# Two-block transformer kernel on one core: bias rows in 32 copies instead of 128, memory tokens loaded earlier, nine weight pages instead of seven at the start

## Chip, core and metric

The kernel runs on one core of a Trainium2 chip. The metric is the device time of one execution in microseconds (us); of several runs the median counts. Engines are named as in the profile: PE (TensorE matmul), PEld (its weight loads), DVE (VectorE), ACT (ScalarE), POOL (GpSimd), SP (SyncE); a "q" behind a name is the engine's instruction queue, where DMAs are issued.

## What is computed

Two blocks on 256 tokens of width 1024, in float32 throughout. Cut to what this case touches, the first block is:

```
h    = rms_norm(x) @ w_in            # q, k, v of two attentions, 512 columns each
oa   = softmax(qa ka^T / 8 + bias[h, bucket(t - s)], causal) va        # 8 heads of 64
ob   = (softmax(.. + bias) - lam * softmax(.. + bias)) vb              # 4 heads, two maps each
x    = x + concat(norm(oa), norm(ob)) @ w_out
m    = rms_norm(mem)                 # 256 memory tokens
x    = x + softmax((rms_norm(x) wq)(m wk)^T) (m wv) wo
x    = x + swiglu(rms_norm(x))
```

The bias of a head depends on the distance t - s alone, so that a row of 384 numbers per head holds all of a head's 256x256 map. A second block follows (gated linear recurrence, spatial gating, routing to 8 of 64 experts) and the final norm; the change leaves both as they are.

## The kernel before

All work is unrolled and its order is the program's order on every engine. SBUF is cut into 25 **pages** of 1 MB (128 partitions x 2048 float32).

**Chunks.** The weights come as a planned stream of 1 MB pages (class Stream, L175 to L274); I call the n-th page of the plan chunk n. Chunks 0 to 11 are w_in, two per 512 columns, in the order k, q, v of the first attention (0 to 5) and k, q, v of the second (6 to 11); chunks 12 to 15 are w_ck, 16 to 19 w_cv, then w_out and the rest. A chunk is loaded (L220), then **converted** by halves: ACT rounds it into a page `wh` (L246) and DVE forms the rest `wl` (L247), two pages in all, and the raw page is free again. A product is three matmuls: with `wh` (L643), with the low part of the other side (L644), with `wl` (L645). A chunk is 48 matmuls of 256 columns (tile `ws`) or 24 of 512 (tile `tsb`).

**What sets the order.** `st.limit(name)` takes from the table CAP (L81) how many pages the stream may hold and how many half chunks may stand converted ahead. `pump` (L202) converts half a chunk if there is room for two pages, then issues loads as long as there is room for one page, and for two more if a loaded chunk is still unconverted (L210). It is called at every `get`, in the middle of a chunk and at every `free`. "start" holds from the beginning until "a1" (3 pages, L983), which is set behind chunk 11; "a2" (7 pages, L975) is set between chunks 13 and 14. At a `free` under "start" the stream of before holds two converted chunks and issues one load.

**Queues.** All loads named here are issued by SP, in program order; the store of the bias rows is issued by ACT. Every DMA of both queues gets one of eight completion semaphores in turn, and one that gets a semaphore again is not issued before the transfer that had it last has landed. So a transfer that takes long holds back the eighth DMA after it, and on the same queue all that stand behind that one.

**The bias.** PE forms the 12 rows of 384 numbers (`bv`, L710), DVE copies them to SBUF (L711), and one DMA writes every row 128 times to DRAM (`bd`, L715) at a pitch of 513, so that reading at a pitch of 512 from offset 127 turns copy p by p places: partition p of the map. Two loads (L778) fetch the maps, `biasA` for 8 heads and `biasB` for 4, behind chunk 5. The store stands on ACT's queue behind the first two of four quarter steps, each of which scales two blocks of xT (`gain`, L580/L581) and converts a quarter of chunk 0 (L575/L576).

**Attention.** The weave "att" (L980) puts the attention steps, the preparation of the memory tokens (`mem_prep`, L897) and the second attention between the half chunks of chunks 6 to 19, at the places in ORDER (L43). The scores `qk` of the first attention come in the middle of chunk 7, the softmax (L809 adds the bias, L811 takes the maximum, L813 the exponentials) behind them, the transposes `pt` (L832) behind chunk 8. The loads of memT and mem (L892, L894) are issued behind the bias maps; they are first read by `mem_prep` in the middle of chunk 8.

```
 210  if src is None or self.room() < 1 + (2 if self._pending() else 0): break
 237  if 2 * self.ready >= self.ahead and force is None or self.room() < 2: break
```

Of the kernel before, what the change touches and what calls it, by code (L numbers as in the profile page):

```python
# [10 lines left out]
F32 = mybir.dt.float32  # L11
# [16 lines left out]
def steps():  # L28
# [7 lines left out]
    for kind in KINDS:  # L36
# [41 lines left out]
        [-1, -1, -1, 3],  # L78
    ],
}  # L80
CAP = {"start": (7, 4), "a1": (3, 8), "a2": (7, 4), "a3": (9, 4), "a4": (11, 3), "out": (10, 2), "cq": (9, 4),  # L81
       "cq1": (8, 5), "cross": (7, 3), "co": (10, 4), "ffn": (12, 3), "ffn_in": (10, 5), "z": (8, 5), "f0": (5, 4),
       "f1": (8, 4), "v": (6, 4), "cm": (6, 4), "gt": (8, 6), "branch": (12, 2), "wo": (14, 4), "post": (11, 3),
       "router": (18, 3)}
# [90 lines left out]
class Stream:  # L175
# [19 lines left out]
    def limit(self, name):  # L195
        self.cap, self.ahead = CAP[name]
        self.pump()
# [83 lines left out]
def run_all(gen):  # L281
    for _ in gen:
        pass
# [40 lines left out]
def body(nc, tc, A, OUT, ctx, dbg=None):  # L324
# [8 lines left out]
    dr = ctx.enter_context(tc.tile_pool(name="dr", bufs=1, space=bass.MemoryType.DRAM))  # L333
    ctx.enter_context(tc.manual_schedule())

    def raw_page(name, dt=F32):
        return pg.tile([128, 2048], dt, tag="pg", name=name, bufs=NP)

    def page(name, dt=F32):
        assert len(live) + st.used + 1 <= NP, (name, [n for n, _ in live.values()], st.used)  # L340
        t = raw_page(name, dt)
        live[id(t)] = (name, t)
        return t
# [15 lines left out]
    def bank(name="bk"):  # L359
        return ps.tile([128, 512], F32, tag="ps", name=name, bufs=8)  # L360
# [23 lines left out]
    def w3(t, **kw):  # L384
        return t.rearrange("p (a b) -> p a b", **kw)
# [78 lines left out]
    oh, bvs = tmp0[0:33, 0:384], tmp0[0:12, 384:768]  # L464
# [35 lines left out]
    def gcol(key):  # L500
        a, n = COL[key]
        return [cols[:, i:i + 1] for i in range(a, a + n)]
# [36 lines left out]
    def rstd2(src, junk):  # L539
        return newton(sumsq(halves(src), halves(junk)), 2, 1024.0)  # L540
# [33 lines left out]
    def split(hi, lo, src):  # L574
        S.activation(hi, src, AF.Copy)  # L575
        V.tensor_sub(lo, src, hi.bitcast(F32))  # L576
# [6 lines left out]
    def gain(parts, xT_, g, ks=range(8)):  # L583

        for k in ks:
            sl = slice(k * 256, k * 256 + 256)
            split_scaled(parts[0][:, sl], parts[1][:, sl], xT_[:, sl], g[k])
# [54 lines left out]
    def mm3(out, l, r, start, stop, free=False):  # L642
        PE.matmul(out, l[0], r[0], start=start, stop=False, skip_group_check=free)  # L643
        PE.matmul(out, l[0], r[1], start=False, stop=False, skip_group_check=free)  # L644
        PE.matmul(out, l[1], r[0], start=False, stop=stop, skip_group_check=free)  # L645


    def ws512(hT, key, c0, evac, need=None):

        hv = [w3(h, a=8) for h in hT]  # L650
        bks = [bank("ws") for _ in range(2)]
        for h in range(2):
            if need:
                need(h)
            c = st.get((key, c0, h))
            wv = [w3(x, a=4) for x in (c.hi, c.lo)]
            for k in range(4):
                for ct in range(4):
                    o = bks[ct // 2][:, (ct % 2) * 256:(ct % 2) * 256 + 256]
                    mm3(o, [x[:, k, ct * 128:ct * 128 + 128] for x in wv], [x[:, h * 4 + k, :] for x in hv],  # L660
                        h == 0 and k == 0 and ct % 2 == 0, h == 1 and k == 3 and ct % 2 == 1, True)
                if k == 1:
                    st.pump()
                    yield
            st.free(c)
            if h == 0:
                yield
        for i in range(2):
            evac(i, bks[i])
        yield  # L670
# [34 lines left out]

    st.cap, st.ahead = CAP["start"]
    c.hi, c.lo = raw_page("wh", F32R), raw_page("wl", F32R)
# [1 line left out]
    bv = bank("bv")  # L709
    PE.matmul(bv[0:12, 0:384], tab, oh, start=True, stop=True)  # L710
    V.tensor_copy(bvs, bv[0:12, 0:384])  # L711
    bd = dr.tile([12, 128, 512], F32, name="bd")
    for i in range(4):
        if i == 2:
            nc.scalar.dma_start(bass.AP(tensor=bd.tensor, offset=bd.offset, ap=[[65536, 12], [513, 128], [1, 384]]),  # L715
                                bvs[:, None, :].to_broadcast([12, 128, 384]))
        s = slice(i * 512, i * 512 + 512)
        gain(hT, xT, gcol("mix_norm_g"), (2 * i, 2 * i + 1))
        split(c.hi[:, s], c.lo[:, s], c.raw[:, s])
# [15 lines left out]
    def evac_q(dst, f):  # L735
        def g(i, b):
            V.scalar_tensor_tensor(w3(dst[:, i * 512:i * 512 + 512], a=2), w3(b, a=2), 0.125, f["row"][:, None, :]
                                   .to_broadcast([128, 2, 256]), op0=OP.mult, op1=OP.mult)
        return g
# [9 lines left out]
    next(unit), next(unit)  # L749
    fx["col"] = rstd2(xp, mixed)  # L750
    run_all(unit)
    unit = ws512(hT, "w_in", 0, evac_q(qkA[:, 0:1024], fx))
    next(unit), next(unit)
    fx["row"] = row_of(fx["col"])
# [20 lines left out]
    rel(tmp0)  # L775
    run_all(ts512(hT, "w_in", 1024, evac_v(vab[:, 0:1024], fx)))
    for t, h0, n in ((biasT[0], 0, 8), (biasT[1], 8, 4)):
        nc.sync.dma_start(w3(t[:, :n * 256], a=n), bass.AP(tensor=bd.tensor, offset=bd.offset + h0 * 65536 + 127,  # L778
                                                           ap=[[512, 128], [65536, n], [1, 256]]))

    def attention(diff, qk_, v, bias, out_cols):
        q, k = w3(qk_[:, 0:1024], a=4), w3(qk_[:, 1024:2048], a=4)
# [105 lines left out]
        yield from turns(mixed, fm["mx"], 8, (gcol("moba_out_g") + gcol("diff_subln_g") * 4), bs=(2, 3) if diff else (0, 1))  # L888


    memT = page("memT")
    nc.sync.dma_start(memT, A["memT"])  # L892
    memx = page("mem")
    nc.sync.dma_start(memx, A["mem"])  # L894
    fm = {}

    def mem_prep():  # L897
# [236 lines left out]
    def ffn_in():  # L1134
        hv = [w3(h, a=8) for h in nh["h"]]
        for u in range(11):
# [4 lines left out]
            for n in ("w_gate", "w_up"):  # L1141
# [3 lines left out]
                for k in range(8):  # L1145
# [5 lines left out]
                    if k == 3:  # L1151
# [18 lines left out]
                                                ap=[[0, 128], [1, 1024]]))  # L1170
# [6 lines left out]
    for u in range(11):  # L1177
# [3 lines left out]
        for tt, k2 in sorted(parts) if u == 10 else parts:  # L1181
            f = 2 * u + k2
            i, o = divmod(f * 256, 2048)
# [977 lines left out]
    bd = [mset.bank("ed") for n in range(2)]  # L2161
# [88 lines left out]
```

## Time and profile before

| | |
|---|---|
| median of 3 runs | 1227.41 us (1226.05 to 1227.77) |
| the profiled execution | 1227.2 us, its span 1225.4 us |
| PE busy, DVE, ACT | 95%, 52%, 38% of the span |
| DMA moved | 353.20 MB, mean 288 GB/s |

The page's busy shares are means over stages that differ much: weights with conversion (to about 757 us), then the experts. A stretch view (from:to in us, busy time and count of each engine, granted clock PEclk, busy share of the DMA engines, GB/s) shows each stage by itself. In a timeline row the first two numbers are start and duration, and square brackets tell the idle time of the engine before it and what ended it. [...]

### The profile page before, as it was taken

To read this page: it belongs to the slowest core of one execution; us is meant where nothing else is said; L and a number is where in the kernel's file an instruction comes from. 1 tells how busy PE (TensorE), PEld (TensorE's weight loads), DVE (VectorE), ACT (ScalarE), POOL (GpSimd) and SP (SyncE) were. 2 spreads that over 40 slices of the span, in tenths; PEclk is the share of its full clock that TensorE was granted. 3 is DMA by queue.
4 is the path that set the end of the run, shared out by engine and by line. 5 is a ranking of instruction groups with operands and counts; after the bars stand their busy time and mean duration, and the time that the engine had idled before them with its cause. 6 is when DMAs were issued, how large, how long until landed. Compare 5 with 4: busy or idle time off the path is not lost.

```text
span 1225.4 us, 18528 instructions
## 1 busy us (share of the span) xinstructions
PE 1166.3 (95%) x7391; PEld 837.5 (68%) x7391; DVE 632.9 (52%) x1280; ACT 465.9 (38%) x738; POOL 2.0 (0%) x9
## 2 busy tenths in 40 slices
PE   7989999999999999999999978999999999998986
PEld 6878987689999988998888757444444434442442
DVE  4568856465545446865686656343333323331333
ACT  4446535545534443777445433111111111110121
POOL 0000000000000000000000000000000000000000
PEclk9889999999999999999999988999999999999998
DMA  8853789644554665343355997899999999999994
GB/s 300 252 213 138 264 344 388 241 174 153 190 206 143 228 226 178 118 149 114 139 193 197 361 359 288 336 410 422 422 420 420 421 421 421 420 421 421 421 420 175
DMA packets 55152, 353.20 MB, mean 288 GB/s; under 512 B 6007, under 2 KB 9368, under 8 KB 13848
## 3 DMA queue, kind: packets, MB, share of 16 engines
q1 hardware_dynamic: 51984, 342.90, 70.7%
q10 hardware_dynamic: 3080, 9.10, 2.6%
q8 instruction: 59, 0.97, 0.3%
q14 instruction: 29, 0.24, 0.1%
HBM read 347.51 MB, written 4.46 MB: 287 GB/s over the span
## 4 chain that ended last, share of the span: by engine, by line
PE 70%; DMA 22%; DVE 4%; ACT 2%; issue 1%; SPq 0%; DVEq 0%; ACTq 0%
DMA w<-in_w_expert_gu 11%; PE gu L1940 8%; DMA w<-in_w_expert_down 6%; PE tsb L643 6%; PE tsb L645 6%; PE tsb L644 6%; PE ed L1969 5%; DMA w<-in_w_in 3%; PE ga L1909 3%; PE acc L1979 3%; PE ws L645 2%; PE ws L643 2%; PE ws L644 2%; PE w_up L643 2%; PE w_gate L643 2%; PE w_up L645 2%
## 5 line engine op out<-in xcount | busy, mean ns | idle before, releaser
L247 DVE TENSOR_TENSOR wl<-w,wh 128x1024 fp32r<-128x1024 f32 (+1 forms) x210 | 242.3, 1201 | 95.9 <-ACT wh L246 87.2
L246 ACT ACTIVATE wh<-w 128x1024 fp32r<-128x1024 f32 (+1 forms) x210 | 205.0, 1039 | 66.6 <-DMA w<-in_w_in 31.8
L1940 PE MATMUL gu<-w,xe 128*32 128x512 f32 (+1 forms) x1216 | 201.3, 594 | 11.8 <-DMA w<-in_w_expert_gu 11.8
L1940 PEld LDWEIGHTS gu<-w,xe 128*32 128x32 f32 (+1 forms) x1216 | 61.1, 121 | 147.5 <-issue 115.2
L1969 PE MATMUL ed<-w,hT 128*32 128x512 f32 (+1 forms) x608 | 109.0, 597 | 3.0 <-DMA w<-in_w_expert_down 2.9
L643 PE MATMUL ws<-hi,wh 128*128 128x256 f32 x352 | 104.1, 296 | 3.2 <-ACT wh L246 3.2
L645 PE MATMUL ws<-hi,wl 128*128 128x256 f32 x352 | 102.7, 292 | 1.6 <-DVE wl L247 1.2
L643 PE MATMUL tsb<-wh,hi 128*128 128x512 f32 x256 | 101.5, 397 | 2.1 <-ACT g1r L572 2.1
L644 PE MATMUL ws<-lo,wh 128*128 128x256 f32 x352 | 102.6, 292 | 0.5 <-DVE lo L581 0.5
L645 PE MATMUL tsb<-wh,lo 128*128 128x512 f32 x256 | 99.9, 390 | 0.0
L644 PE MATMUL tsb<-wl,hi 128*128 128x512 f32 x256 | 99.9, 390 | 0.0
L1949 DVE TENSOR_TENSOR hh<-hh,gu 128x256 f32<-128x256 f32 x27 | 11.4, 422 | 148.3 <-ACT hh L1948 148.3
L580 ACT ACTIVATE ey<-ed,ws 128x512 fp32r<-128x512 f32 x54 | 37.1, 687 | 122.4 <-PE ed L1969 122.4
L1948 ACT ACTIVATE hh<-gu 128x256 f32<-128x256 f32 x27 | 10.4, 383 | 188.2 <-PE gu L1940 188.2
L581 DVE SCALAR_TENSOR_TENSOR ey<-ed,ws,ey 128x512 fp32r<-128x512 f32 x54 | 40.5, 751 | 77.7 <-ACT ey L580 77.7
L643 PEld LDWEIGHTS ws<-hi,wh 128*128 128x128 f32 x352 | 70.6, 201 | 6.2 <-ACT wh L246 3.8
L1969 PEld LDWEIGHTS ed<-w,hT 128*32 128x32 f32 (+1 forms) x608 | 29.8, 121 | 64.8 <-issue 50.0
L645 PEld LDWEIGHTS ws<-hi,wl 128*128 128x128 f32 x352 | 70.3, 200 | 2.4 <-DVE wl L247 1.7
L644 PEld LDWEIGHTS ws<-lo,wh 128*128 128x128 f32 x352 | 70.5, 200 | 0.9 <-DVE lo L581 0.8
L1979 PE MATMUL acc<-ey,gt 128*128 128x512 f32 x216 | 60.0, 412 | 0.0
L643 PEld LDWEIGHTS tsb<-wh,hi 128*128 128x128 f32 x256 | 48.2, 188 | 11.8 <-ACT g1r L572 2.5
L1979 PEld LDWEIGHTS acc<-ey,gt 128*128 128x128 f32 x216 | 37.5, 188 | 27.4 <-issue 21.4
(450 smaller groups left out, 2116.5 us busy)
## 6 DMA issues: line engine op xcount, KB each, us to landing
w<-in_w_expert_gu SPq DMA_DIRECT2D x128, 1024.0 KB, 19.8
w<-in_w_expert_down SPq DMA_DIRECT2D x60, 1024.0 KB, 19.7
w<-in_w_in SPq DMA_DIRECT2D x39, 1024.0 KB, 7.0
w<-in_w_ada SPq DMA_DIRECT2D x24, 1024.0 KB, 7.2
w<-in_w_gate SPq DMA_DIRECT2D x11, 1024.0 KB, 4.9
w<-in_w_up SPq DMA_DIRECT2D x11, 1024.0 KB, 6.5
w<-in_w_down SPq DMA_DIRECT2D x11, 1024.0 KB, 5.0
w<-in_w_out SPq DMA_DIRECT2D x8, 1024.0 KB, 6.7
```

Source lines behind the costliest of these rows:

```text
L246: kb.nc.scalar.activation(c.hi[:, s], c.raw[:, s], AF.Copy)
L247: kb.nc.vector.tensor_sub(c.lo[:, s], c.raw[:, s], c.hi[:, s].bitcast(F32))
L580: S.activation(hi, src, AF.Copy, scale=col)
L581: V.scalar_tensor_tensor(lo, src, col, hi.bitcast(F32), op0=OP.mult, op1=OP.subtract)
L643: PE.matmul(out, l[0], r[0], start=start, stop=False, skip_group_check=free)
L644: PE.matmul(out, l[0], r[1], start=False, stop=False, skip_group_check=free)
L645: PE.matmul(out, l[1], r[0], start=False, stop=stop, skip_group_check=free)
L1909: PE.matmul(b[:, i * w:i * w + w], xs[part][:, tt, dd * 128:dd * 128 + 128], oh_[:, tt, :], start=part + tt == 0, stop=part + tt == 2)
L1940: PE.matmul(b[w * e:w * e + w, :], xe[:, k, w * e:w * e + w], w3(gu[e][k // 4], a=4)[:, k % 4, :], start=k == 0, stop=k == 7, skip_group_c ...
L1949: V.tensor_mul(h, h, b[:, 256:512])
L1969: PE.matmul(b[w * e:w * e + w, :], hT_[:, f * 128 + w * e:f * 128 + w * e + w], w3(dn[e], a=2)[:, f, n * 512:n * 512 + 512], start=f == 0, ...
L1979: PE.matmul(sums[tt, n], gt[:, tt * 128:tt * 128 + 128], y[:, part * 1024 + n * 512:part * 1024 + n * 512 + 512], start=False, stop=stop a ...
```

## The change

The bias rows are written in 32 copies (a quarter of the bytes), ahead of the four quarter steps instead of behind the second; the maps are read in four parts of 32 partitions each, with the offset moved for each part. The two loads of the memory tokens move from behind the bias maps to behind chunk 1. "start" grows from 7 pages to 9.

```
-CAP = {"start": (7, 4), ...
+CAP = {"start": (9, 4), ...
...
-    bd = dr.tile([12, 128, 512], F32, name="bd")
+    bd = dr.tile([12, 32, 512], F32, name="bd")
+    nc.scalar.dma_start(bass.AP(tensor=bd.tensor, offset=bd.offset, ap=[[16384, 12], [513, 32], [1, 384]]),
+                        bvs[:, None, :].to_broadcast([12, 32, 384]))
     for i in range(4):
-        if i == 2:
-            nc.scalar.dma_start(bass.AP(tensor=bd.tensor, offset=bd.offset, ap=[[65536, 12], [513, 128], [1, 384]]),
-                                bvs[:, None, :].to_broadcast([12, 128, 384]))
         s = slice(i * 512, i * 512 + 512)
         gain(hT, xT, gcol("mix_norm_g"), (2 * i, 2 * i + 1))
         split(c.hi[:, s], c.lo[:, s], c.raw[:, s])
...
     fx["col"] = rstd2(xp, mixed)
     run_all(unit)
+    memT = page("memT")
+    nc.sync.dma_start(memT, A["memT"])
+    memx = page("mem")
+    nc.sync.dma_start(memx, A["mem"])
     unit = ws512(hT, "w_in", 0, evac_q(qkA[:, 0:1024], fx))
...
     for t, h0, n in ((biasT[0], 0, 8), (biasT[1], 8, 4)):
-        nc.sync.dma_start(w3(t[:, :n * 256], a=n), bass.AP(tensor=bd.tensor, offset=bd.offset + h0 * 65536 + 127,
-                                                           ap=[[512, 128], [65536, n], [1, 256]]))
+        for q in range(0, 128, 32):
+            nc.sync.dma_start(w3(t[q:q + 32, :n * 256], a=n),
+                              bass.AP(tensor=bd.tensor, offset=bd.offset + h0 * 16384 + 127 - q,
+                                      ap=[[512, 32], [16384, n], [1, 256]]))
...
-    memT = page("memT")
-    nc.sync.dma_start(memT, A["memT"])
-    memx = page("mem")
-    nc.sync.dma_start(memx, A["mem"])
```

## Rows read from the trace of the kernel before

**Rows 1.** The page: the span, and the chain that ended last by engine.

```profile
span 1225.4 us, 18528 instructions
...
PE 70%; DMA 22%; DVE 4%; ACT 2%; issue 1%; SPq 0%; DVEq 0%; ACTq 0%
```

**Rows 2.** Stretches: from:to, length, busy us of engines (count), PEclk, DMA share, GB/s.

```profile
8.60:13.60 5.00, 5.00 (x23) 5.00 (x24) 4.30 (x9) 2.75 (x6) 0.00 (x0) 1.00 1.04 416
13.60:28.30 14.70, 14.70 (x123) 14.46 (x121) 7.78 (x20) 5.54 (x10) 0.00 (x0) 1.00 0.99 325
28.30:31.50 3.20, 0.01 (x1) 0.00 (x0) 0.02 (x1) 1.11 (x2) 0.00 (x0) 0.88 0.75 312
31.50:37.50 6.00, 5.54 (x24) 5.24 (x25) 5.34 (x6) 4.27 (x6) 0.00 (x0) 0.50 0.74 224
72.80:75.90 3.10, 0.00 (x0) 0.00 (x0) 3.03 (x5) 1.80 (x4) 0.00 (x0) 0.87 0.64 196
75.90:81.90 6.00, 5.97 (x23) 4.55 (x24) 3.57 (x7) 6.00 (x24) 0.00 (x0) 0.50 0.18 78
115.10:117.20 2.10, 0.01 (x1) 0.03 (x1) 1.89 (x7) 2.10 (x7) 0.00 (x0) 1.00 0.90 378
...
930.00:1193.00 263.00, 248.24 (x1457) 111.28 (x1457) 83.63 (x234) 47.77 (x81) 0.00 (x0) 1.00 1.01 421
```

**Rows 3.** The SP queue's waits to 60 us: total us, times, longest.

```profile
SPq L220 <- DMA bd<-tmp: 25.1, 1, 25.1
```

**Rows 4.** Timeline of SP: the last load before that wait, the first three after.

```profile
19.96 0.33 SPq L220 DMA_DIRECT2D w<-in_w_in  x1
...
45.45 1.28 SPq L220 DMA_DIRECT2D w<-in_w_in  x3
```

**Rows 5.** DMA queues in 12:18, 20:26 (two), 36:44, 54:60; q10 is ACT's, q1 SP's.

```profile
q10 hardware_dynamic: 216, 0.33, 14.6%
...
q10 hardware_dynamic: 330, 0.51, 62.1%
q1 hardware_dynamic: 412, 0.86, 37.0%
...
q10 hardware_dynamic: 405, 0.62, 67.2%
...
DMA packets 1656, 2.16 MB, mean 360 GB/s; under 512 B 48, under 2 KB 1584, under 8 KB 1584
```

**Rows 6.** The chain in order of time: start, us from issue to landing, load.

```profile
13.98 16.39 DMA w<-in_w_in
...
54.41 14.80 DMA w<-in_w_in
```

**Rows 7.** Timelines of ACT, DVE and PE at the start.

```profile
4.91 0.91 ACT L580 ACTIVATE hi<-xT,cols 128x256 fp32r<-128x256 f32 x2 [1.44 <-DMA xT<-in_xT]
...
6.59 0.55 DVE L711 COPY tmp<-bv 12x384 f32<-12x384 f32 x1 [5.69 <-PE bv L710]
...
8.59 0.58 PE L645 MATMUL ws<-hi,wl 128*128 128x256 f32 x1 [0.42 <-DVE wl L576]
```

**Rows 8.** Timelines of PE, ACT, DVE and PE around the first softmax.

```profile
61.36 2.58 PE L798 MATMUL qk<-qkA 64*128 64x128 f32 x24
...
69.23 2.01 ACT L246 ACTIVATE wh<-w 128x1024 fp32r<-128x1024 f32 x2 [9.59 <-DMA w<-in_w_in]
...
72.60 0.69 DVE L809 TENSOR_TENSOR pp<-qk,biasA 128x512 f32<-128x512 f32 x1
...
75.93 3.17 PE L832 MATMUL pt<-misc,pp 128*128 128x128 f32 x8 [3.17 <-ACT pp L813]
```

**Rows 9.** Timelines of PE, ACT and DVE behind chunk 13, where chunk 14 begins.

```profile
125.08 1.04 PE L598 MATMUL tr<-misc,mixed 128*128 128x128 f32 x8
...
125.78 1.57 ACT L623 ACTIVATE hi<-tr,cols 128x256 fp32r<-128x256 f32 x4 [0.62 <-PE tr L598]
...
124.23 1.23 DVE L247 TENSOR_TENSOR wl<-w,wh 128x1024 fp32r<-128x1024 f32 x1 [2.11 <-ACT wh L246]
```

More of the change, by code (lines that the diff above doesn't have):

```diff
@@ L80 @@
 }
-CAP = {"start": (7, 4), "a1": (3, 8), "a2": (7, 4), "a3": (9, 4), "a4": (11, 3), "out": (10, 2), "cq": (9, 4),
+CAP = {"start": (9, 4), "a1": (3, 8), "a2": (7, 4), "a3": (9, 4), "a4": (11, 3), "out": (10, 2), "cq": (9, 4),
        "cq1": (8, 5), "cross": (7, 3), "co": (10, 4), "ffn": (12, 3), "ffn_in": (10, 5), "z": (8, 5), "f0": (5, 4),
```

## Prediction

> **What bounds the kernel now.** I read the page first: PE makes 70% of the chain that ended last and DMA 22% [rows 1]. The stretches say where each rules. From 930 to 1193 us the DMA engines are full at 421 GB/s while PE has idle time [rows 2]; up to the routing, some 170 us earlier, PE is the bound. The expert loads that fill the DMA engines can only follow the routing, which stands at the end of the PE-bound part. So time saved on PE early in the program should move routing, expert loads and end by the same amount, and the question is what PE loses in the first 130 us, the only part that the change touches.
>
> [...] The start is slow too: 23 matmuls in 5.0 us before 13.6, 123 in 14.7 us after (0.22 against 0.12 us each); the 1.00 printed for that first stretch isn't borne out by this spacing.
>
> Next the SP queue's waits: one load waited 25.1 us for `bd` [rows 3], between 19.96 and 45.45 [rows 4]. That load does not read `bd`; it is the eighth DMA after the store. Everything behind it on SP came late: biasA, biasB, memT, mem and chunks 6 to 11. The chain of waits shows the two loads that hurt [rows 6]: chunk 3, issued at 13.98, landed at 30.37, and chunk 9, issued at 54.41, landed at 69.21. ACT stood 9.59 us before chunk 9's conversion, DVE's softmax (72.60) was queued behind that conversion, and PE's transposes waited 3.17 us for the softmax [rows 8].
>
> **The change part by part**, against the profiled 1227.2 us (0.2 below the median).
>
> *The store in 32 copies.* 1536 packets become 384. ACT's queue moved 405 packets in 8 us when alone and 216 in 6 us beside SP's loads [rows 5], 51 and 36 per us. So 384 take 7.6 to 10.7 us; begun near 11.5 us (an estimate, from the packet rate behind the issue) they end near 21.5 instead of 45. The 25 us wait goes. In its place an earlier DMA waits for `bd`: the store takes its semaphore some places earlier, so the last small load or chunk 3 is held to about 21.5. That costs little, as the transfers that SP has issued by then keep the engines busy till about that time.
>
> *What chunk 3 gains.* In 20:26 SP's small loads (misc, lambda and two bias tables) shared the engines with `bd`, which held 62.1% of them against 37.0% [rows 5]. Without it those 6 us shrink to some 3, and chunk 3 lands near 27; bounds are 26 and the 30.4 of before. Its first half then stands converted (1.0 us on ACT, 1.2 on DVE, [rows 8, 9]) at 29.3.
>
> *The store moved ahead of the quarter steps.* ACT began them at 4.91; now its queue first waits for DVE's copy of the rows, which ends at 7.14 [rows 7]. With 0.3 us to issue it begins at 7.5, 2.6 us later. DVE and PE wait for ACT there: PE's third matmul needs two gains (0.91), a split (0.6) and a subtraction (0.7), so comes at 9.8 instead of 8.59 [rows 7]. 1.2 us at the low clock are 0.7 us of work at the high one. Bounds: 0.7, and 2.4 if the clock rises that much later. Chunk 2, which ended at 28.3, ends near 29.0.
>
> So the first term: idle 3.2 + 0.46, half of 5.54 busy us at 0.50 (2.8), and a wait of 0.76 that PE has at 52 us for the first load behind the store, less 0.7 and a rest of 0.3 before chunk 3: **6.2 us**, from 1.5 to 7.5.
>
> *Nine pages, tokens earlier.* Each load is now issued two chunks earlier in the program. The order on SP is chunks 3 to 6, memT, mem, 7 to 10, the bias parts, 11. A page at 421 GB/s takes 2.5 us [rows 2], so from 27 on chunk 9 lands at 47 and chunk 10 at 49.5. Moving 2 MB of tokens ahead costs chunk 7 on 5 us each, which it can bear: chunk 7 lands at 42 and PE wants it converted near 52. ACT no longer stands before chunk 9 and the softmax starts when the scores are there. The idle 3.17 and half of 5.97 us at 0.50 (3.0) go. Of the 2.1 us at 115 I count half: there DVE has four passes of 0.69 and the difference of the maps to do while PE has half a chunk. Second term: **7.3 us**, from 4 to 9.
>
> *The maps in four parts.* Eight loads instead of two, six more issues of about 0.4 us on SP, which has waits to spare there. 1656 mostly small packets moved in 6 us [rows 5], 276 per us; biasA has 1024, so it lands at 49.5 + 3.7 = 53.2 and biasB at 55. The scores stood at 61.36 [rows 8], less 6.2 is 55.2, and the first add comes some 1.6 us behind. Cost nil; the cover is the 3.6 us, and behind it the time till the transposes are wanted (72.8 - 6.2 = 66.6, less 3.3 us from first add to first transpose in [rows 8]): 63.3.
>
> *The cap at "a1".* This price isn't in any row of before. At "a1" the stream now holds 7 pages instead of 5 (two converted chunks and three raw, where it was one). Chunks 12 and 13 free four, so 3 are left instead of 1. Under the cap of 3 there is room for 0 pages instead of 2, and a conversion wants 2 (L237). So chunk 14 isn't converted at chunk 13's `free` as before but after "a2": on DVE behind both `kmT` evacuations, on ACT behind the four `hi` of the mixer's turns, all of which need chunk 13's end. By [rows 9] PE's turns end at 126.12, ACT's `hi` at 127.35; half a conversion is 1.0 on ACT, then 1.23 on DVE: 129.6. PE loses **3.5 us**. Such a wait was followed by 6 us at 0.50 where it was 3.2 and 3.1 us long, not where it was 2.1; I take the low clock, another **3.0 us**. Bounds 0 and 6.5.
>
> Sum: 6.2 + 7.3 - 3.5 - 3.0 = 7.0; 1227.2 - 7.0 = 1220.2, and 0.2 more for the median: **1220.4 us**.
>
> **Rivals.** *No low clock, or a shorter wait, at chunk 14:* 1217.4, down to 1213.9 with no wait. For it: PE's wait is broken by two matmuls, as none of the others was.
>
> *The start gives little:* chunk 3 lands near 29.5 and PE's clock rises later, so the first term is its low bound, 1.5: 1225.1. For it: ACT's 2.6 us delay; against it, `bd`'s 62.1% of the engines.
>
> *The maps come late:* parts of 32 partitions move slowly and the first softmax waits again. At 51 packets per us (the store out of 12 partitions, the low bound of [rows 5]) biasA takes 20.2 us and lands at 69.7, 6.4 us after 63.3; with the low clock 9.4 us are lost: 1229.8. It turns the sign where biasA lands after 67.3, below 58 packets per us. Against it: the nearest row has 276, with the same bytes per packet. [...]
>
> *The store stays slow*, so the change doesn't do what it says: were its time not set by its packets, chunk 3 would be held until 45 instead of 20. Chunk 3 lands about 5.5 us behind `bd`, so beyond 26 us for `bd` the kernel is slower (the other terms leave 0.8), and at 45 it takes 1247. The steady 51 packets per us speak against it.
>
> **Numbers.** Forecast 0.46, no low clock 0.30, weak start 0.14, maps late 0.06, store slow 0.04. The range 1213.5 to 1224.7 holds the first two and half of the third. A measurement of this kernel tells 0.2% (2.5 us) from no change: faster than 1225.0 are the first two and most of the third, 0.85; same 0.08; slower 0.07.
>
> **What would show it.** Right: no wait of SP for `bd` over 10 us; no PE idle over 1 us near 29 and before `pt`; ACT's first gain near 7.5; PE idle of 3 to 4 us before chunk 14, near 112, ended by `wl`, and 0.50 behind it; the last 400 us the same but shifted. Wrong: chunk 3 landing after 30, biasA after 63, or PE time won early and lost again before routing.

## The result, and the profile after

The changed kernel takes 1220.34 us (median of 5 runs, 1219.54 to 1221.89) against 1226.48 for the kernel before beside it: ratio 0.9941, 95% interval 0.993 to 0.9952 (the quotient of the two medians is 0.9950, inside the interval). The profiled execution took 1219.82 us, its span 1218.0, which is 7.4 less than before [rows 1]. Line numbers of the changed kernel are up to five higher.

First the page of the changed kernel: the span, and the chain by engine.

```profile
span 1218.0 us, 18537 instructions
...
PE 69%; DMA 26%; DVE 2%; ACT 1%; issue 1%; SPq 0%; ACTq 0%; DVEq 0%
```

PE's share of the chain fell by one point and DMA's rose by four. The stretches of the changed kernel (columns as in [rows 2]):

```profile
13.60:28.80 15.20, 15.18 (x127) 14.94 (x125) 7.78 (x20) 5.89 (x11) 0.00 (x0) 1.00 0.75 285
28.80:30.90 2.10, 0.58 (x3) 0.38 (x3) 1.36 (x2) 1.66 (x2) 0.00 (x0) 1.00 1.01 425
30.90:36.90 6.00, 6.00 (x48) 5.92 (x49) 5.70 (x7) 4.29 (x5) 0.00 (x0) 1.00 1.01 427
...
112.10:115.70 3.60, 0.62 (x4) 0.34 (x3) 2.20 (x4) 3.60 (x7) 0.00 (x0) 1.00 0.84 291
116.10:119.50 3.40, 3.40 (x18) 3.40 (x17) 3.40 (x4) 3.40 (x5) 0.00 (x0) 0.50 0.39 128
```

The 3.2 us hole at 28.3 is down to two short ones with the clock at 1.00 behind them (48 matmuls in 6.0 us where there were 24); the new hole is the one at 112, with 0.50 behind it. What ended PE's waits, by line, from 9 to 150 us:

```profile
PE ws L643 <- ACT wh L246: 3.0, 2, 2.2
PE ws L643 <- ACT wh L575: 2.5, 1, 2.5
PE ws L645 <- DVE wl L247: 1.5, 2, 0.8
PE pt L837 <- DVE pp L833: 0.8, 1, 0.8
```

No wait for the first attention's transposes is left (3.17 us in [rows 8]). The SP queue's waits to 60 us, and its timeline, where the store went out on ACT at 6.80:

```profile
SPq L494 <- DMA bd<-tmp: 10.8, 1, 10.8
```

```profile
9.86 0.33 SPq L492 DMA_DIRECT2D tmp<-in_diff_lambda  x1
21.03 0.33 SPq L494 DMA_DIRECT2D bsp<-in_b_spatial  x1
21.41 0.50 SPq L496 DMA_DIRECT2D brow<-in_b_router  x1
21.95 2.11 SPq L220 DMA_DIRECT2D w<-in_w_in  x4
```

The 25.1 us of [rows 3] are 10.8 now, but the load that waits is a small one ahead of chunk 3, and chunk 3 goes out at 21.95 instead of 13.98 [rows 6].

### The profile page after: what moved, and what is told of

Its sections match the earlier page's. It is cut to its first block, busy times and chain, and to the rows that moved or that the text cites. A ratio compares the mean times of both kernels' runs of the same rounds, so it can differ in the third digit from the quotient of the medians.

```text
span 1218.0 us, 18537 instructions
## 1 busy us (share of the span) xinstructions
PE 1162.6 (95%) x7391; PEld 836.0 (69%) x7391; DVE 633.5 (52%) x1280; ACT 465.9 (38%) x738; POOL 2.0 (0%) x9
## 4 chain that ended last, share of the span: by engine, by line
PE 69%; DMA 26%; DVE 2%; ACT 1%; issue 1%; SPq 0%; ACTq 0%; DVEq 0%
DMA w<-in_w_expert_gu 15%; DMA w<-in_w_expert_down 8%; PE tsb L643 6%; PE tsb L645 6%; PE tsb L644 6%; PE gu L1941 6%; PE ed L1970 3%; PE ws L645 3%; PE ws L643 3%; PE ws L644 3%; PE ga L1910 2%; PE acc L1980 2%; PE w_up L643 2%; PE w_gate L643 2%; PE w_gate L644 2%; PE w_up L644 2%
## 5 line engine op out<-in xcount | busy, mean ns | idle before, releaser
L246 ACT ACTIVATE wh<-w 128x1024 fp32r<-128x1024 f32 (+1 forms) x210 | 204.8, 1039 | 45.9 <-DMA w<-in_w_in 12.3
```

Of the source, the lines that this page charges most:

```text
L246: kb.nc.scalar.activation(c.hi[:, s], c.raw[:, s], AF.Copy)
```

## The experiments

Twelve kernels ran, in three sets of four, each set with runs of the kernel before beside it on the same chip. That median was 1227.7 to 1228.3 us in the sets and 1226.48 in the result above, so between sets the ratios are the fairer comparison. Every profile has three marks on PE by which the stages can be told apart: the first attention's scores (61.36 us before, 56.06 changed), the first turn of the mixer's output behind chunk 13 (125.08, 111.14), and adaT, PE's first product behind w_cv and w_ada (194.46, 185.53).

**Store alone, and pages with tokens alone.** The first run takes the other two parts out of the changed kernel, the second puts only them into the kernel before.

```
 CAP "start": (7, 4)          # first run; (9, 4) in the second
 memT, mem                    # first run: loaded behind the maps; second: behind chunk 1
 bd                           # first run: 32 copies, ahead; second: 128 copies, old place
```

> The changed kernel with the start cap back at 7 pages and memT and mem back behind the bias maps: of the change only the store in 32 copies, its place ahead of the quarter steps and the maps in four parts remain. Theory A (everything the change gains comes from the short store, since the late load of chunk 9 was itself a result of the SP queue held for 25 us; the nine pages only bring the new wait at chunk 14): no PE idle over 1 us near 29 and before pt, chunk 13 ending within 1 us of the 111.3 of the changed kernel, and no PE idle over 1 us behind it, since three raw chunks' worth of pages isn't held there; 5 us of the wait and low clock at 112 to 119 go, so 1213.5 to 1216. Rival B (my prediction's second term: the pages and the early tokens are what brings chunk 9 in time): PE idle of 2 to 3 us before pt with a low clock behind it comes back, chunk 13 ends near 118, and the time is 1220 to 1224.

> The kernel before with the start cap at 9 pages and memT and mem issued behind chunk 1, but with the old store of 128 copies and two bias loads: the other half of the change alone. Theory A (the short store carries the gain): SP's load still waits about 25 us for bd, PE is idle 3 us near 29 with a low clock behind it; the wait before pt goes, as loads are issued two chunks earlier, which gives up to 7 us from 73 to 82, but the wait of PE behind chunk 13 of some 2 to 3 us and its low clock come, 5 us; 1224 to 1227. Rival B (pages and tokens carry the gain, the store is hidden): near the changed kernel, 1219 to 1222.

Store alone: 1215.82 us, 0.9907 (0.9894 to 0.992), faster than the whole change. Pages and tokens alone: 1230.49, 1.0017 (1.0007 to 1.0027), slower than before, and above what I had expected. PE's waits in the same stretch, of the one (behind its start), then of the other:

```profile
PE pt L833 <- DVE pp L829: 2.0, 1, 2.0
PE ws L645 <- DVE wl L247: 0.8, 1, 0.8
PE ws L643 <- ACT wh L246: 0.5, 1, 0.5
```

```profile
PE ws L643 <- ACT wh L246: 7.0, 4, 3.8
PE ws L645 <- DVE wl L247: 2.7, 4, 0.8
PE pt L836 <- DVE pp L832: 2.0, 1, 2.0
PE o L853 <- DVE nv L511: 1.4, 1, 1.4
```

In the first, the wait before the first attention's transposes is gone with seven pages and late tokens: a shorter store is enough to bring chunk 9 in time. The turns behind chunk 13 came at 113.04, 1.9 us behind the changed kernel and not within 1 us as A had said, as PE's wait before the second attention's transposes is still 2.0 us. In the second the wait before the first transposes goes too, so either half of the change is enough for that; but chunk 3 is as late as before (3.8 us for 3.2), chunk 7, behind the token loads, is now late (0.6 and 0.8 us at 59), one more wait of 1.4 us stands at 81, and the wait at chunk 14 (2.2 and 0.8 us) is there. My 1224 to 1227 had left out the waits at 59 and 81.

**The wait at chunk 14.** Two ways to take it away: seven pages, or a higher limit behind chunk 11.

```
-CAP = {"start": (9, 4), "a1": (3, 8), ...
+CAP = {"start": (7, 4), "a1": (3, 8), ...      # first run
+CAP = {"start": (9, 4), "a1": (5, 8), ...      # second run
```

> The changed kernel with the start cap at 7 pages, all else as changed (tokens early). Theory A (the wait of 2.2 and 0.8 us and the low clock at 112 to 119.5 come from the two converted chunks and three raw ones that nine pages leave at the limit of 3 behind chunk 11; with seven pages one raw chunk less is held and chunk 14 is converted at chunk 13's end): no PE idle over 1 us between 100 and 125, and 1213.5 to 1216. Rival B (nine pages are needed: without them chunks 7 to 9 are late, as the two token loads are ahead of them): PE idle over 1 us between 50 and 80, 1219 or more.

> The changed kernel with one number changed: the limit behind chunk 11 is 5 pages instead of 3, so that chunk 14's first half is converted when chunk 13's pages come free, with nine pages at the start as in the change. Theory A (the wait at chunk 14 is the limit's and nothing else's): PE idle near 112 falls from 2.2 and 0.8 us to below 1 us, PEclk stays 1.00 there, 3 to 5 us less than the changed kernel: 1215 to 1217. Rival B (the wait is for ACT and DVE, whose work on the maps and the mixer stands before the conversion in any case): the idle time stays within 0.5 us and so does the time, 1219.5 to 1221.

1214.63 us, 0.9895 (0.9881 to 0.991), and 1216.10, 0.9901 (0.9887 to 0.9916). No wait over 1 us stands at chunk 14 in either, so the wait needs both the nine pages and the limit of 3. In the first a wait of 1.79 us stands before the second attention's transposes, which its expectation (none over 1 us from 100 to 125) had left out. PE's waits of the second run, behind its start:

```profile
PE ws L643 <- ACT wh L246: 1.9, 1, 1.9
PE pt L837 <- DVE pp L833: 0.8, 1, 0.8
PE ws L645 <- DVE wl L247: 0.5, 1, 0.5
```

The 1.9 is at 29.25: in this execution the store went out 0.45 us later than in the changed kernel (7.25 instead of 6.80), and chunk 3's wait grew by 1.1 us and brought a low clock of 6.8 us. So the start of the changed kernel stands near an edge.

The marks give the price of that wait cleanly. From the turns to adaT nine profiles need 69.36 to 69.39 us: all with seven pages, the kernel before among them, and the two with the limit of 5. The five with nine pages and the limit of 3 need 72.9 to 74.4 (the changed kernel 74.39). So the wait, its low clock and what follows cost the changed kernel 5.0 us up to adaT.

**The place of the store, and its size.**

```
 for i in range(4):
+    if i == 2:                                     # first run: the store of 32 copies here again
+        nc.scalar.dma_start(... [513, 32] ...)
-bd = dr.tile([12, 32, 512], ...)
+bd = dr.tile([12, 64, 512], ...)                   # second run: 64 copies, two parts of 64
```

> The changed kernel with the store of 32 copies back behind the second quarter step. Theory A (SP is still held until the store lands, 14 us behind its issue in the changed kernel; an issue 2 to 4 us later moves the landing of bd from 20.9 to 23 to 25 and chunk 3's from 28.4 to 31 to 32, while chunk 2 ends some 0.6 us earlier): PE idle of 3 to 4 us near 29 with a low clock of some 6.8 us behind it, 4 to 6 us more than the changed kernel, 1224 to 1226. Rival B (chunk 3 lands when the DMA engines have worked off what was issued before, wherever the store stands): chunk 3 lands within 1 us of 28.4 and the time is 1219 to 1221.

> The changed kernel with 64 copies of the bias rows and the maps read in two parts of 64 partitions: the suspected cost of the store, its packets, doubled. Theory A (the store's time goes by its packets and holds SP): 768 packets land bd at 27 to 30 instead of 20.9, chunk 3 at 34 to 37 instead of 28.4, PE is idle 5 to 8 us there and at the low clock behind it, 1227 to 1231. Rival B (the store's time isn't set by its packets, or SP's wait is hidden): bd lands within 2 us of 20.9 or PE's idle time stays under 2 us, 1219 to 1222. Beside it: if the four parts were slow because each went into 32 partitions, a part of 64 partitions takes about as long for twice the bytes (1.2 us a part in the changed kernel).

The first result is against my theory A and against B: 1216.27 us, 0.9899 (0.9884 to 0.9914), 4 us less than the changed kernel (5 by the ratios). Its SP timeline, and its wait for `bd`:

```profile
11.32 0.33 SPq L494 DMA_DIRECT2D bsp<-in_b_spatial  x1
11.95 0.33 SPq L496 DMA_DIRECT2D brow<-in_b_router  x1
14.43 7.00 SPq L220 DMA_DIRECT2D w<-in_w_in  x4
```

```profile
SPq L220 <- DMA bd<-tmp: 0.7, 1, 0.7
```

The store went out at 7.50, only 0.7 us later than in the changed kernel, since there ACT first had to wait for DVE's copy, which ended at 6.77. What differs most is the turn it takes among the eight semaphores, counted here from which load waits for `bd` (the one of L494 for 10.8 us there, one of L220 for 0.7 here). Ahead of the quarter steps it stands before xT's last part, and the eighth DMA behind it is a small load ahead of chunk 3. Behind the second step it stands behind x, and the eighth is chunk 6, which is not in a hurry. ACT's quarter steps also begin at 5.09 instead of 7.22, PE's first wait of 2.5 us for ACT is gone, and the scores come at 53.45 instead of 56.06. This lead of 2.6 to 2.7 us is still there at adaT (182.84 for 185.53). The kernels below with the store at this place issue it at 6.92 to 9.25 and have the scores at 52.82 to 53.32: the issue time hardly matters among them.

With 64 copies: 1227.94, 0.9998 (0.9987 to 1.0008), within A.

```profile
SPq L494 <- DMA bd<-tmp: 17.3, 1, 17.3
```

```profile
PE ws L643 <- ACT wh L246: 9.6, 2, 7.3
```

The hold (SP's wait for `bd`) ended at 27.47 instead of 21.03: 384 more packets took 6.4 us, 60 per us. PE waited 7.35 us for chunk 3 instead of 0.78. Doubling the store gives back all that the change brings.

**Another queue, and another order on SP.**

```
-            nc.scalar.dma_start(... [513, 128] ..., bvs ...)      # first run: kernel before
+            for g in range(0, 128, 32):
+                nc.gpsimd.dma_start(... offset=bd.offset + g * 513, [513, 32] ..., bvs ...)
 ...
+    memT, mem, then dl, bsp, brow       # second run: changed kernel, 7 pages, small loads here
```

> The kernel before with one thing changed: its store of 128 copies is issued by POOL in four DMAs of 32 copies each, at its old place, and so takes no turn among the eight semaphores of SP's and ACT's DMAs. Packets, bytes and the two loads of the maps stay. Theory A (what cost the time was SP's wait for bd, not the packets): no wait of SP for bd below 25 us, chunk 3 lands at 24 to 28, PE idle under 1 us near 29 and before pt; 1213 to 1217. Rival B (1536 packets take the DMA engines' time from chunk 3 whoever issues them): chunk 3 lands after 30, PE idle over 2 us near 29, 1221 or more. A third outcome, if POOL's issue is itself slow: bd lands after 55, the maps are late and PE waits over 2 us before pt.

> The changed kernel with the start cap at 7, as in the run without nine pages, and the three small loads (lambda, spatial bias, router bias) moved behind chunk 1 and the token loads, so that chunks 3 and 4 come before them on SP and chunk 4, not a small load ahead of chunk 3, is the eighth DMA behind the store. Theory A (chunk 3 is still late only because it stands behind a load that waits for bd): chunk 3 is issued by 11 and lands at 22 to 26, the idle times of 0.5 and 0.8 us at 29 to 31 go, some 1.3 us less than that run's 1214.6: 1212.5 to 1214. Rival B (until 21 the DMA engines are full, and chunk 3 comes behind what they hold or slows the loads of x and the constants, for which the row scale waits): no gain, 1214 to 1216.

From POOL: 1225.80 us, 0.9977 (0.9967 to 0.9987), nearest to the third outcome. Chunk 3 landed at 25.63 and PE had no wait over 0.45 us from 9 to 60. But POOL's timeline shows the four stores one after the other, the last out at 42.90, landing at 52.76 (I had written after 55); SP then stood before biasA, which reads `bd`, and chunk 9 was late again (POOL's timeline, then the waits of SP and of PE):

```profile
30.57 0.67 POOL L716 DMA_DIRECT2D bd<-tmp  x1 [10.98 <-issue]
42.90 0.67 POOL L716 DMA_DIRECT2D bd<-tmp  x1 [11.65 <-issue]
```

```profile
SPq L780 <- DMA bd<-tmp: 25.7, 2, 15.6
...
PE pt L834 <- ACT pp L815: 9.5, 1, 9.5
```

What each kernel did with 20:26, when chunk 3 should come, in the order: before (its line of all queues, whose shares are in [rows 5]), changed, behind the second step, from POOL:

```profile
DMA packets 743, 1.38 MB, mean 230 GB/s; under 512 B 235, under 2 KB 634, under 8 KB 654
```

```profile
DMA packets 443, 0.76 MB, mean 127 GB/s; under 512 B 303, under 2 KB 357, under 8 KB 364
```

```profile
DMA packets 615, 2.53 MB, mean 421 GB/s; under 512 B 231, under 2 KB 306, under 8 KB 326
```

```profile
DMA packets 771, 2.37 MB, mean 395 GB/s; under 512 B 309, under 2 KB 405, under 8 KB 563
q0 software_dynamic: 120, 0.36, 19.0%
```

These are three different limits. Before, the engines were busy with `bd` (62.1%); in the changed kernel they had little to do (127 GB/s), since SP stood; behind the second step they were full of weights (421 GB/s). From POOL the store came in 120 packets (0.36 MB, 19%) where it had 330 (0.51 MB, 62.1%), so that run doesn't tell the hold from the packets. The same store of 32 copies at two places does, but for ACT's earlier quarter steps; the next run tells these two apart.

With the small loads moved: 1214.81, 0.9889 (0.9874 to 0.9904), against 0.9895 with seven pages and the old order. Chunk 3 went out at 9.87, landed at 23.59, and both waits at 29 are gone, as A said; the scores came 2.0 us earlier (54.46 against 56.44). But PE's wait before the second attention's transposes was 2.04 us instead of 1.79 and had 3.4 us at 0.50 behind it, and at the next wait, 0.72 us at 181, the lead was 0.1 us. B's time, by another way than B's. The store stands in its new place here, so the 2.0 us at the scores come from chunk 3 no longer standing behind the hold. With the store behind the second step and seven pages (below) the scores come at 52.82, another 1.6 us earlier, and there ACT's quarter steps are no longer delayed.

**The repairs together.**

```
 e9:  kernel before, + 32 copies at the old place, + maps in four parts
 e10: changed kernel, store behind the second step, "a1": (5, 8)
 e12: changed kernel, store behind the second step, "start": (7, 4)
```

> The kernel before with the store in 32 copies at its old place and the maps read in four parts, and nothing else of the change: seven pages, tokens behind the maps. Theory A (the whole gain is the shorter store; its new place ahead of the quarter steps costs 2.5 to 3 us, because there the load that waits for bd stands ahead of chunk 3, and nine pages cost the wait at chunk 14): no PE idle over 0.5 us between 10 and 60, none over 1 us before pt of the first attention or at chunk 14; 2.5 to 3 us less than the run of the store alone with its new place (1215.8), 1212 to 1214. Rival B (time won in the first 60 us is given back at the second attention's transposes, where PE waits 2 us for DVE, as in the run with the small loads moved): 1214.5 to 1216.5.

> The changed kernel with the store back behind the second quarter step and the limit behind chunk 11 at 5 pages: the two repairs that each gave about 4 us alone. Theory A (they remove different waits, the ones at 29 to 31 and at 112 to 119): both waits gone, the idle before the second attention's transposes at 0.8 us as with nine pages, 1211 to 1213. Rival B (one wait: what is won at the start is lost again at chunk 14 or later): 1215 or more.

> The changed kernel with the start cap at 7 and the store behind the second quarter step; the tokens stay early. Theory A: 2.5 to 3 us less than the run without nine pages (1214.6), 1211.5 to 1213, with the early tokens worth under 1 us against the run of the copies alone. Rival B (the 2 us wait before the second attention's transposes grows by what is won before it, or brings a low clock of 3 to 7 us): 1214 to 1216.

1214.39 us, 0.9883 (0.9868 to 0.9898); **1210.97, 0.9865 (0.9849 to 0.988)**; 1212.27, 0.987 (0.9855 to 0.9885). The first is 0.4 above A's range and just under B's. The second beats both kernels and is as A forecast, at its lower edge: the two waits were different ones. The third is within A, but its median is 2.1 us below the first's where A had said under 1; the two intervals overlap. Of the second: the only wait of PE that the view lists from 9 to 150 us, and two stretches:

```profile
PE pt L838 <- DVE pp L834: 0.8, 1, 0.8
```

```profile
13.60:28.80 15.20, 15.20 (x129) 15.20 (x129) 10.43 (x23) 8.95 (x14) 0.00 (x0) 1.00 1.03 421
...
108.00:120.00 12.00, 12.00 (x103) 12.00 (x102) 11.82 (x14) 9.95 (x13) 0.00 (x0) 1.00 0.84 306
```

Compare the DMA column of the first line: 421 GB/s where the changed kernel has 285. The other two have seven pages, and in both profiles the 2 us wait before the second attention's transposes is followed by 3.4 us at 0.50 (the second half of the third run's B): part of what they won is lost there (the third's profile is of its slowest run, 1215.43). With nine pages that wait is 0.8. The marks show this in all profiles with a shorter store on ACT's queue: from the scores to the turns the six with nine pages need 55.1 us, the five with seven 56.0 to 58.8. So nine pages win 0.9 to 3.7 us there, and lose about 5 us behind it unless the limit at "a1" lets chunk 14 be converted. In the times of whole runs the second kernel's lead over the other two is less sure: the intervals of the ratios overlap. Seven pages with the limit of 5 were not run.

**The order of the parts.**

```
-        for q in range(0, 128, 32):
+        for q in (0, 64, 32, 96):
```

> The changed kernel with one line changed: the parts of each map are read in the order 0, 64, 32, 96 instead of 0, 32, 64, 96. [...] In both cases the time is the changed kernel's, 1219 to 1222, as PE waits for no map. [...]

1218.47 us, 0.9929 (0.9915 to 0.9942): 0.5 us under the 1219 to 1222 of its expectation, and not told from the changed kernel (0.993 to 0.9952). BiasA's parts landed from the load before them in 3.96 us (53.21 to 57.17), against 4.48 in the changed kernel (53.28 to 57.76). No run shows where these 0.5 us come from. The rates while maps move: before 55.2:58.4, changed 53.5:57, 64 partitions 60:63.5, in turn 53.5:57.

```profile
DMA packets 1106, 1.12 MB, mean 349 GB/s; under 512 B 16, under 2 KB 1106, under 8 KB 1106
```

```profile
DMA packets 815, 0.81 MB, mean 230 GB/s; under 512 B 70, under 2 KB 809, under 8 KB 809
```

```profile
DMA packets 768, 0.78 MB, mean 224 GB/s; under 512 B 37, under 2 KB 763, under 8 KB 763
```

```profile
DMA packets 863, 0.88 MB, mean 252 GB/s; under 512 B 79, under 2 KB 852, under 8 KB 852
```

Parts of 64 partitions were no faster per byte than parts of 32 (224 against 230 GB/s; biasA's second part of 64 landed 2.4 us behind the first, for 1.2 us a part of 32), and the order 0, 64, 32, 96 won, with 252, a little of the way to the 349 of 128 partitions.

## Why the prediction was right, step by step

The time was 1220.34 for 1220.4. The terms have about the sizes that I gave them, the second for a cause that was right only in part. That the sum fits to 0.1 us is luck: three terms were off by about 1 to 1.5 us each, a loss later in the program was missing, and these cancelled; and the kernel before measured 1226.48 beside the result, not the 1227.41 that the sum started from. Two of the named signs went the other way: SP's wait for `bd` was 10.8 us, over the 10 that I allowed, and 1.5 of PE's lead were lost again before routing.

- **The store:** `bd` landed at about 21 for "near 21.5"; in the run with the store doubled 384 more packets took 6.4 us, 60 per us where I had 51, and its queue moved 266 in 5.5 us nearly alone (21.5:27), 48 per us. Right. So was that the hold falls on a small load ahead of chunk 3 (it is the spatial bias, the last but one).
- **"That costs little":** wrong. I took the engines as busy until the hold ends. They were until 20 (388 GB/s from 14 to 20), but then had little queued: 127 GB/s from 20 to 26. Chunk 3 landed at 28.45, not 27. This and the delay of the quarter steps I had at 1.0 (0.7 and 0.3); the store at its old place gives 2.6 at the scores. The first term was 6.2; measured 5.3 (scores 61.36 to 56.06).
- **The second term:** 7.3, measured 8.6. The turns behind chunk 13 begin at 111.14 (first row of the fence further below) for 125.08 in [rows 9], 13.94 in all, less 5.3 is 8.64. The 3.17 us, the low clock behind it and 1.25 of the 2.1 before the second transposes (2.09 to 0.84) are in it. But I gave it to the pages and the tokens, and the run of the store alone has no wait before the first transposes either. The size was about right, the cause only in part: chunk 9 was late because SP was held, the short store alone mends that, and what the nine pages add to it is the shorter wait before the second transposes (0.84 us, for 1.79 with seven pages and early tokens).
- **The maps:** biasA landed at 57.76 for 53.2, biasB at 60.04 for 55. Most of the 4.6 us is chunk 10, the load before them, which landed at 53.28 for 49.5; biasA then took 4.48 us for 3.7. For that I had the packet rate of 128 partitions, 276 per us; parts of 32 took 1.22 us per 256 packets, 210 per us. In GB/s, parts of 32 moved 230 against 349 with 128 partitions, two thirds, and parts of 64 moved 224. The first add stood right behind biasA's last part, 1.78 us behind the scores (1.19 with the halves in turn), and the cover held:

```profile
57.84 0.69 DVE L814 TENSOR_TENSOR pp<-qk,biasA 128x512 f32<-128x512 f32 x1 [2.38 <-PE qk L803]
```

  DVE idled, PE did not.
- **The cap at "a1":** place, instruction and cause right: nine pages leave chunk 14 unconverted, and it is converted behind the mixer's `hi`. The timelines of PE and ACT there:

```profile
111.14 1.03 PE L598 MATMUL tr<-misc,mixed 128*128 128x128 f32 x8
...
114.40 0.39 PE L643 MATMUL ws<-hi,wh 128*128 128x256 f32 x1 [2.23 <-ACT wh L246]
...
115.66 0.39 PE L645 MATMUL ws<-hi,wl 128*128 128x256 f32 x1 [0.76 <-DVE wl L247]
```

```profile
111.83 1.57 ACT L623 ACTIVATE hi<-tr,cols 128x256 fp32r<-128x256 f32 x4 [2.17 <-PE tr L598]
113.27 4.85 ACT L246 ACTIVATE wh<-w 128x1024 fp32r<-128x1024 f32 x5
```

  2.23 and 0.76 are 3.0 us for my 3.5; the clock was at 0.50 for 3.4 us, 1.7 lost (an estimate, half of it), for my 3.0. The term was 6.5; these rows give 4.7, the mark at adaT 5.0. Seven pages or the limit of 5 take it away.
- **"The last 400 us the same but shifted":** not quite. At its first product behind w_cv and w_ada (adaT, 185.53 for 194.46) PE was 8.9 us ahead; 1.5 of that was lost later, as the span is only 7.4 shorter. The stretches of the changed kernel at 676 and 717:

```profile
675.90:679.30 3.40, 3.40 (x9) 2.67 (x8) 3.33 (x6) 1.06 (x2) 0.00 (x0) 0.51 1.01 424
716.80:727.00 10.20, 4.53 (x21) 4.54 (x22) 3.88 (x17) 3.73 (x5) 0.00 (x0) 0.50 1.02 429
```

  Before, nothing below 1.00 stood at the first, and 6.8 us at 0.50 at the second. So the early terms were 0.4 too small, the cap's 1.5 too dear, and 1.5 went later where I had nothing: 7.0 predicted, 7.4 in the span.

The loss behind adaT can be placed. Seven of the fourteen profiles have 3.4 us at 0.50 somewhere from 669 to 689 us, and in each of these seven 3.4 us at 0.50 stood between 103 and 128 before it. Of the other seven only the one with the small loads moved has the early stretch. Behind adaT the seven with the late stretch take 1031.8 to 1033.0 us (the changed kernel 1032.5), the seven without it 1029.7 to 1031.3 (before 1030.9). That is near 1.7 us, my estimate (half of it) for what 3.4 us at 0.50 cost. The run with the limit of 5, which has every part of the change, has 1.00 from 660 to 690. So the late stretch doesn't come with the changed code, but in seven of eight profiles it followed a low clock at chunk 14 or behind the second transposes. What stays open is why: no run shows how the early stretch brings the late one, or why the clock falls where it does.

## What to carry to other kernels

Here a long DMA cost what stood behind the DMA that took its semaphore again: SP stood 25.1 us [rows 3] for the store of 128 copies, 10.8 for 32 ahead of the quarter steps, 0.7 for 32 behind the second. Count which DMA that is at each place the long one could stand, before you judge a place by its issue time: behind the second step the store went out 0.7 us later and the kernel was 4 us faster, and 2.0 us of that is the hold's, by the scores in the run with the small loads moved. A reserve of loaded pages is only worth what the next limit lets through: nine pages cost 4 to 6 us behind a limit of 3 and gave the lowest time behind a limit of 5.

## What I had not expected of the hardware

- The length of a wait didn't alone tell whether the clock fell. In the profiles here, 2.09 us before the second transposes (kernel before) had 1.00 behind it, 1.94 at the same place in the run of the copies alone had 3.4 us at 0.50; 1.86 us at 673 in the changed kernel had 3.4 us, 2.11 us in the kernel before none.
- A store of 1536 rows from 12 partitions, issued by POOL in four, went one part after the other: the last two went out 11.6 and 12.3 us behind the ones before them, and the map loads had to wait for all four.
